# Differential attention of a two-block network: projection groups 1, 6 and 7 run tile by tile beside the sixteen attention units, with the group and output orders changed

## The chip, the cores and the metric

The program runs on one core of one Trainium2 chip. The metric is the device time of one execution in microseconds (us), taken as the median of several executions. The core has TensorE (PE, with its weight loads shown apart as PEld), VectorE (DVE), ScalarE (ACT), GpSimd (POOL) and SyncE (SP, which issues most loads). Each engine works through its own list of instructions in order and waits for the others by semaphores.

## What is computed

The kernel runs two transformer blocks on 256 tokens of width 1024, in float32. The part around the change is the first mixer of the second block. Cut to what matters:

```python
def mixer_ab(hx, hc, w_in, w_out, ...):
    q_x, k_x, v_x, gu_x, gv_x = split(hx @ w_in)      # widths 1024, 1024, 1024, 512, 512
    q_x, k_x = apply_rope(q_x), apply_rope(k_x)       # 8 heads of 2 x 64
    k_c, v_c = split(hc @ w_in[:, 1024:3072])         # 256 context tokens
    k_all, v_all = concat([k_c, k_x]), concat([v_c, v_x])
    s = einsum('bqhmd,bkhmd->bhmqk', q, k) * 64 ** -0.5
    p = softmax(s)
    o_x = (p[:, :, 0] - lam * p[:, :, 1]) @ v         # differential attention, 8 heads
    a_x = head_rms(o_x)                               # width 1024
    u, v = gelu(gu_x), layer_norm(gelu(gv_x))
    g_x = u * (w_s @ v + b_s)                         # the gate, width 512
    return concat([a_x, g_x]) @ w_out                 # 1536 x 1024
```

Ahead of it stands the first block (windowed attention and a gated feed-forward layer); behind it come a layer norm, an expert layer (PEER), a pooling mixer and a second PEER layer. They are the same in both kernels.

## The kernel before

**Products.** A float32 weight tile of 128x1024 is loaded by SP into a `raw` buffer (five of them) and split in two parts: `hilo` (L197 to L200) makes the high part `hi` with an ACT copy (L199) and the rest `lo` with a DVE subtraction (L200; POOL for the few tiles that the plan marks). Each product then takes three matmuls. Weight tiles follow one list, `_plan` (L81). `W.use` (L71) hands out the next tile and, with its default look-ahead of 2, first splits the tiles up to two places further on. So the instructions for splitting a tile are issued when the tile two places before it is used. There are three `hi` and three `lo` buffers.

**The AB projections.** `w_in` is cut into eight groups of 512 columns, four tiles each: 0 and 1 are the queries, 2 and 3 the keys, 4 and 5 the values, 6 and 7 the two halves `gu` and `gv` of the gate. `AB_ORDER` (L117) is their order. `ab_group` (L1044) is a generator that does one tile per step: 24 matmuls of 128x512 for a group with context tokens (2 to 5), 12 for the others. Each step also runs one or two entries of a list `todo` through `do_next` (L1013). `ab_evac` (L1017) puts a finished group's remaining work on that list: the rotary products on DVE and POOL and the transpositions on PE (L988 to L1009) for queries and keys, copies for values, `Gelu` on ACT (L1041) for the gate. `AB_PUMPS` (L114) says in which groups a step also does a piece of `ada`, a modulation product on DVE with a load of its own (L318).

**The gate.** `gate_steps` (L1107) is a generator of seven steps: two loads, a layer norm of `gv` for each half of the tokens on DVE (L508 to L1118), two steps of matmuls and DVE products (L1123, L1125), two of transpositions and splits (L1134).

**The attention.** A loop over `u` from 0 to 21 (L1267) is a software pipeline written out by hand. A unit is one head and one half of the queries. Unit `u` issues, in this order: squares of an earlier head (ACT), `d_scale` of u-1 (reciprocal and product with lambda on DVE L1198, L1199, then a scaled copy on ACT L1200), `d_scores` of u (four passes of matmul into two PSUM banks L1179, two maxima on DVE L1183, L1184), output and norm of earlier heads (`d_out`, `d_on`, L1252 and L1238), `d_mix` of u-1 (DVE L1205), `d_transpose` of u-2 (PE L1212, ACT copy L1214), `d_values` of u-3 (PE L1224), `d_exp` of u (two `Exp` on ACT L1191), and in every other unit `d_flip` (PE L1250). In u from 16 to 21 the attention drains, and eight of the twelve tiles of `w_out` are multiplied there (L240 to L244), in the order of `AB_OUT_ORDER` (L118); the last four follow behind the loop (L267 to L269). All matmul results lie in eight PSUM banks, handed out by the framework as they come free.

Before, seven groups run ahead of the loop, with the gate's steps put on `todo` when group 7 is done, and the last group (1, the queries of heads 4 to 7) runs in units 0 to 3:

```python
for gidx, g in zip(AB_ORDER[:-1], groups):   # L1154
    for _ in g:
        pass
    if gidx == 7:
        gate = gate_steps()
        todo.extend([lambda: next(gate, None)] * 7)
```

Of the kernel before, what the change touches and what calls it, by code (L numbers as in the profile page):

```python
# [2 lines left out]

# [77 lines left out]
def _plan(t):  # L81

    p = [(("q", j), t["att_q"][j], None) for j in range(8)]
    p += [(("o", k), t["att_o"][k], "big" if k >= 8 - O_TAIL else None) for k in range(8)]
    for j in range(FFT):
        p += [(("fi", j, z), t["ffn_in"][z * FFT + j], None) for z in range(2)]
    p += [(("fo", k), t["ffn_out"][k], None) for k in range(FFT)]
    for g in AB_ORDER:
        p += [(("ab", g, k), t["ab_in"][g, k], "pool" if g == AB_ORDER[-1] else None) for k in range(4)]

    p += [(("abo", k), t["ab_out"][k], BIG[AB_OUT_ORDER.index(k) % 2] if k in AB_OUT_ORDER[-TAIL:] else None) for k in AB_OUT_ORDER]
    for li in range(2):
        if li == 1:
            p += [(("pi", k), t["pool_in"][k], "pool" if k == 0 else None) for k in range(8)]
            p += [(("pg", k), t["pool_grp"][k], "big") for k in range(2)]
            p += [(("po", k), t["pool_out"][k], BIG[k % 2] if k >= 8 - TAIL else None) for k in range(8)]
        p += [(("wn", li, k), t["wn"][li, k], "pool" if k == 0 else None) for k in range(8)]
        p += [(("wq", li, g), t["wq"][li, g - 8], "pool" if g in Q_POOL else None) for g in range(8, 16)]

        def u(a, b):  # L100
            return [(("u", li, e), t["u"][li, e], None) for e in range(a, b)]

        def v(a, b):
            return [(("v", li, e), t["v"][li, e], BIG[e % 2] if e >= P - TAIL else None) for e in range(a, b)]

        p += u(0, 112) + v(0, 16) + u(112, 128) + v(16, 128)
    return p


TAIL = 4  # L110
NEXT = 3
O_TAIL = 2
BIG = ("big", "big")
AB_PUMPS = (1,) * 7 + (0,)  # L114
KEEP = 2
ADA_AT = 36
AB_ORDER = (2, 0, 6, 7, 3, 4, 5, 1)  # L117
AB_OUT_ORDER = (8, 9, 10, 11, 0, 1, 2, 3, 4, 5, 6, 7)  # L118
Q_POOL = (9, 12, 15)
Q_ORDER = ((8,), (9, 0), (10, 1), (11, 2), (12, 3), (13, 4), (14, 5), (15, 6, 7), ())  # L120
G_STEP = 1.4
# [3 lines left out]
def tile_two_blocks(ctx: ExitStack, tc: tile.TileContext, t: dict, taps=None):  # L125
# [20 lines left out]
    vec, act, pool, pe, dma = nc.vector, nc.scalar, nc.gpsimd, nc.tensor, nc.sync.dma_start  # L146
# [13 lines left out]
    def mm(shape):  # L160
        n = int(np.prod(shape[1:]))
        v = ps_mm.tile([P, 512], F32, tag="mm", name="mm")[:, 0:n]
        return v.rearrange("p (a b) -> p a b", b=shape[2]) if len(shape) == 3 else v
# [5 lines left out]
    def s1(n=256, dt=F32):  # L169
        return p_s1.tile([P, 512], dt, tag="s1", name="s1")[:, 0:n]  # L170
# [27 lines left out]
    def hilo(src, hi, lo, eng=None):  # L198
        act.activation(out=hi, in_=src, func=AF.Copy)  # L199
        (eng or vec).tensor_tensor(out=lo, in0=src, in1=hi.bitcast(F32), op=OP.subtract)  # L200
# [3 lines left out]
    def split(r, eng):  # L204
# [9 lines left out]
        return hi, lo  # L214

    W = _Weights(_plan(t), load, split)


# [13 lines left out]
    def gemm_n(acc, sT, w, first, last, halves=(0, 1)):  # L232

        (sh, sl), (wh, wl) = sT, w
        cs = [slice(c * 512, c * 512 + 512) for c in range(2)]
        for hf in halves:
            o = acc[hf * 2:hf * 2 + 2]
            tk = slice(hf * P, hf * P + P)
            for c in range(2):
                pe.matmul(o[c], lhsT=sh[:, tk], rhs=wh[:, cs[c]], start=first, stop=False)  # L240
            for c in range(2):
                pe.matmul(o[c], lhsT=sh[:, tk], rhs=wl[:, cs[c]], start=False, stop=False)  # L242
            for c in range(2):
                pe.matmul(o[c], lhsT=sl[:, tk], rhs=wh[:, cs[c]], start=False, stop=last)  # L244

    def ramp(left, tail):

        if tail < TAIL:
            return LOOK if left > tail else left
        return min(left + NEXT - 1, LOOK + max(0, tail + 4 - left))  # L250
# [252 lines left out]
    def ln_stats(src):  # L503
        n = src.shape[-1]
        k = n // 512
        st_ = p_c8.tile([P, 2, 6], F32, tag="st", name="st")
        for i in range(k):
            vec.bn_stats(out=st_[:, i, :], in_=src[:, i * 512:i * 512 + 512])  # L508
        mv = sm(2)
        vec.bn_aggr(out=mv, in_=st_[:, 0:k, :])  # L510
        r = sm(1)
        rsqrt(r, mv[:, 1:2], LN_EPS)
        return mv[:, 0:1], r
# [172 lines left out]
    acc = [mm([P, 512]) for _ in range(2)]  # L686
# [195 lines left out]
    acc = acc_o  # L882
# [75 lines left out]
    acc = [mm([P, 512]) for _ in range(4)]  # L958
# [52 lines left out]
    todo = []  # L1011

    def do_next():  # L1013
        if todo:
            todo.pop(0)()
# [86 lines left out]
    cat = {}  # L1102
# [4 lines left out]
    def gate_steps():  # L1107

        sws = s1(512).rearrange("p (g c) -> p g c", c=P)
        dma(out=sws, in_=t["sgu_w"])  # L1110
        ln = ccrow
        dma(out=ln, in_=t["sgu_ln"].partition_broadcast(P))
        yield
        for hf in range(2):
            mu, rs = ln_stats(gv[:, hf, :])
            vec.tensor_scalar(out=gv[:, hf, :], in0=gv[:, hf, :], scalar1=mu, scalar2=rs, op0=OP.subtract, op1=OP.mult)
            vec.tensor_tensor(out=gv[:, hf, :], in0=gv[:, hf, :], in1=ln[:, 0:512], op=OP.mult)
            vec.tensor_tensor(out=gv[:, hf, :], in0=gv[:, hf, :], in1=ln[:, 512:1024], op=OP.add)  # L1118
            yield
        for hf in range(2):  # L1120
            b = mm([P, 4, P])
            for g in range(4):
                pe.matmul(b[:, g, :], lhsT=sws[:, g, :], rhs=gv[:, hf, g * P:g * P + P], start=True, stop=True)  # L1123
            for g in range(4):
                vec.scalar_tensor_tensor(out=gu[:, hf, g * P:g * P + P], in0=b[:, g, :],  # L1125
                                         scalar=cols[:, C_SGUB + g:C_SGUB + g + 1],
                                         in1=gu[:, hf, g * P:g * P + P], op0=OP.add, op1=OP.mult)
            yield
        for g2 in range(2):
            b = mm([P, 2, NTOK])  # L1130
            for i in range(2):
                g = g2 * 2 + i
                for hf in range(2):
                    pe.transpose(b[:, i, hf * P:hf * P + P], gu[:, hf, g * P:g * P + P], ident)  # L1134
            s = slice(4 + g2 * 2, 6 + g2 * 2)
            hilo(b, c1[:, s, :], c1[:, 8 + s.start:8 + s.stop, :])
            yield

    hT = hT_tiles()
    groups = [ab_group(gidx, pumps, 2 * (gidx == AB_ORDER[0])) for gidx, pumps in zip(AB_ORDER, AB_PUMPS)]  # L1140
    gemm_tail(acc, tail, 0)
# [9 lines left out]
    next(groups[0])  # L1151
    T_out(bs, sc, sh, hT, "ab_hx")

    for gidx, g in zip(AB_ORDER[:-1], groups):  # L1154
        for _ in g:
            pass
        if gidx == 7:
            gate = gate_steps()
            todo.extend([lambda: next(gate, None)] * 7)
        if gidx == 4:  # L1160
            lam_prep()
            iota_f = t4(512)
            dma(out=iota_f, in_=t["iota"])
# [98 lines left out]
    acc = None  # L1262
    c2 = big_T(F32R)[0]
    for i in range(4):
        cat[4 + i] = (c2[:, i, :], c2[:, 4 + i, :])
    ab_out = list(AB_OUT_ORDER)
    for u in range(16 + 6):  # L1267
        if u == 16:
            grow = row_pe(mod2[:, 16:24])
        if u == 7:  # L1270
            while todo:
                do_next()
        if u < 4:
            next(groups[-1])
        elif u < 7:
            do_next()
        if at(u, 5) is not None:
            d_squares(at(u, 5))
        if 0 <= u - 1 < 16:
            d_scale(u - 1)  # L1280
        if u < 16:
            d_scores(u)
        if at(u, 7) is not None:
            d_out(at(u, 7))
        if at(u, 6) is not None:
            d_on(at(u, 6))
        if 0 <= u - 1 < 16:
            d_mix(u - 1)
        if 0 <= u - 2 < 16:
            d_transpose(u - 2)  # L1290
        if 0 <= u - 3 < 16:
            d_values(u - 3)
        if u < 16:
            d_exp(u)
        if at(u, 5) is not None:
            d_rms(at(u, 5))
        for _ in range((2, 2, 1, 1, 1, 1)[u - 16] if u >= 16 else 0):
            if acc is None:
                acc = [mm([P, 512]) for _ in range(4)]
            k = ab_out.pop(0)  # L1300
            gemm_n(acc, cat[k], W.use(("abo", k), ramp(len(ab_out) + 1, TAIL)), k == 8, False)
        if at(u, 6) is not None:
            d_flip(at(u, 6))
    scsh = ln_fold(0, mod2)
# [409 lines left out]
    acc = zacc  # L1714
# [32 lines left out]
    for q in range(2):  # L1747
        wh, wl = [x.rearrange("p (g k e) -> p g k e", k=2, e=NTOK) for x in W.use(("pg", q), 1 - q)]
        for gg in range(2):
            g = q * 2 + gg  # L1750
# [9 lines left out]
    acc = [mm([P, 512]) for _ in range(4)]  # L1760
# [105 lines left out]
```

## Time and profile before

| | us |
|---|---|
| median of 3 executions | 2323.43 |
| lowest, highest | 2318.09, 2325.98 |
| the profiled execution | 2319.79 |
| its span, first to last instruction | 2318.0 |
| last two groups of 12-matmul steps ahead of the keys (6 and 7) | 24.3 |
| from the first scores to the drain (16 units) | 62.6 |
| from the drain to the last four tiles of `w_out` | 27.9 |

A row of the timeline gives start, duration, engine, line, operation and tiles of an instruction; neighbours that are alike are merged (x2 and more). A matmul's duration includes its way through the array, so that matmuls which follow each other overlap, and the distance between two starts is what one costs. On ACT and DVE, too, the next instruction starts a little before the row of the last one ends; the text goes by distances of starts.

### The profile page before, as it was taken

The numbers are of one execution on the slowest core, as the hardware profiler recorded it, in microseconds if no ns is written. First come the engines' busy times: TensorE is split into PE (matmuls) and PEld (weight loads), VectorE is DVE, ScalarE is ACT, GpSimd is POOL, SyncE is SP. The second block draws the span as 40 slices with busy tenths as digits, with TensorE's granted clock in tenths as the row PEclk, the third lists the DMA queues.
The fourth block names the chain that finished last, engine by engine and source line by source line (L and its number), as shares of the span: only waits on it lengthen the run. The fifth ranks groups of instructions, "written<-read, shape, count | busy, mean of one in ns | idle before, by whom it ended". The sixth has DMA issues, their size and how long they took to land. (4 is left out here: it accounts for less than half of the span.)

```text
span 2318.0 us, 37641 instructions
## 1 busy us (share of the span) xinstructions
PE 2235.9 (96%) x14766; PEld 1980.6 (85%) x14766; DVE 1650.6 (71%) x2816; ACT 1161.4 (50%) x1692; POOL 118.8 (5%) x103
## 2 busy tenths in 40 slices
PE   6989999989999999999999999999999999999998
PEld 4669988866799999988888887899999998988886
DVE  3658878646699788776777667779877755566666
ACT  3764444357454555434444445554455544444443
POOL 0000001020400000000000002130000000000001
PEclk8999999999999999999999999999999999999999
DMA  8777786522466687898898766555677777778774
GB/s 329 235 236 254 250 271 225 202 82 59 168 195 188 226 273 256 278 331 266 288 310 287 246 215 226 203 164 187 193 243 241 249 229 220 212 237 249 240 245 154
DMA packets 205057, 531.13 MB, mean 229 GB/s; under 512 B 16496, under 2 KB 84624, under 8 KB 204752
## 3 DMA queue, kind: packets, MB, share of 16 engines
q1 hardware_dynamic: 195632, 495.15, 65.6%
q10 hardware_dynamic: 9248, 33.59, 4.5%
q8 instruction: 115, 1.88, 0.3%
q14 instruction: 62, 0.51, 0.1%
HBM read 491.93 MB, written 36.75 MB: 228 GB/s over the span
## 5 line engine op out<-in xcount | busy, mean ns | idle before, releaser
L200 DVE TENSOR_TENSOR lo<-raw,hi 128x1024 fp32r<-128x1024 f32 x655 | 806.1, 1234 | 469.0 <-ACT hi L199 467.1
L199 ACT ACTIVATE hi<-raw 128x1024 fp32r<-128x1024 f32 x668 | 706.7, 1059 | 791.5 <-PE mm L244 349.0
L225 PE MATMUL mm<-hTh,lo 128*128 128x256 f32 x2592 | 737.2, 284 | 10.8 <-DVE lo L200 8.8
L223 PE MATMUL mm<-hTh,hi 128*128 128x256 f32 x2592 | 746.9, 288 | 0.5 <-ACT hTh L458 0.5
L224 PE MATMUL mm<-hTl,hi 128*128 128x256 f32 x2592 | 735.6, 284 | 0.5 <-DVE hTl L460 0.5
L225 PEld LDWEIGHTS mm<-hTh,lo 128*128 128x128 f32 x2592 | 498.0, 192 | 14.8 <-DVE lo L200 12.3
L223 PEld LDWEIGHTS mm<-hTh,hi 128*128 128x128 f32 x2592 | 498.0, 192 | 2.9 <-issue 2.1
L224 PEld LDWEIGHTS mm<-hTl,hi 128*128 128x128 f32 x2592 | 498.5, 192 | 0.8 <-issue 0.6
L242 PE MATMUL mm<-lo,s 128*128 128x512 f32 x992 | 305.8, 389 | 1.8 <-DVE lo L200 1.7
L240 PE MATMUL mm<-hi,s 128*128 128x512 f32 x992 | 305.6, 389 | 0.0
L244 PE MATMUL mm<-hi,s 128*128 128x512 f32 x992 | 305.5, 389 | 0.0
L242 PEld LDWEIGHTS mm<-lo,s 128*128 128x128 f32 x992 | 186.1, 188 | 41.3 <-DVE lo L200 2.6
L244 PEld LDWEIGHTS mm<-hi,s 128*128 128x128 f32 x992 | 186.1, 188 | 39.0 <-DVE s L200 0.3
L240 PEld LDWEIGHTS mm<-hi,s 128*128 128x128 f32 x992 | 185.8, 188 | 38.4
L1498 ACT ACTIVATE t<-mm 128x512 f32<-128x512 f32 x128 | 75.6, 593 | 90.3 <-DMA gspill<-t 44.5
L1480 DVE TENSOR_TENSOR t<-t,pk 128x1024 f16<-128x1024 f16 x128 | 88.6, 692 | 4.4
L1491 PE MATMUL mm<-t 128*128 128x128 f16 x1024 | 79.6, 220 | 9.7 <-DVE t L1480 9.5
L1477 DVE TENSOR_TENSOR t<-pk,iota 128x1024 f16<-128x1024 f16 x128 | 87.6, 685 | 1.2 <-PE mm L1491 0.7
L200 DVE TENSOR_TENSOR s<-big,s 128x512 fp32r<-128x512 f32 x126 | 86.1, 683 | 0.0
L1523 DVE TENSOR_TENSOR big<-t,big 128x1024 f32<-128x1024 f32 x64 | 77.8, 1218 | 6.0 <-DMA t<-gspill 6.0
L318 DVE SCALAR_TENSOR_TENSOR raw<-raw,t 128x1024 f32<-128x1024 f32 x56 | 68.3, 1220 | 17.0 <-DMA raw<-in_ada_dram 12.6
L200 POOL TENSOR_TENSOR lo<-raw,hi 128x1024 fp32r<-128x1024 f32 x13 | 32.3, 2483 | 900.4 <-ACT hi L199 900.4
(290 smaller groups left out, 2356.9 us busy)
## 6 DMA issues: line engine op xcount, KB each, us to landing
raw<-in_u_dram SPq DMA_DIRECT2D x256, 512.0 KB, 4.3
raw<-in_v_dram SPq DMA_DIRECT2D x256, 512.0 KB, 4.4
raw<-in_ada_dram SPq DMA_DIRECT2D x96, 512.0 KB, 4.6
gspill<-t ACTq DMA_DIRECT2D x64, 512.0 KB, 3.3
t<-gspill SPq DMA_DIRECT2D x64, 512.0 KB, 5.6
raw<-in_ffn_in_dram SPq DMA_DIRECT2D x44, 512.0 KB, 4.4
raw<-in_ada1n_dram SPq DMA_DIRECT2D x32, 512.0 KB, 4.1
raw<-in_ab_in_dram SPq DMA_DIRECT2D x32, 512.0 KB, 4.6
```

The source lines that it names most:

```text
L199: act.activation(out=hi, in_=src, func=AF.Copy)
L200: (eng or vec).tensor_tensor(out=lo, in0=src, in1=hi.bitcast(F32), op=OP.subtract)
L223: pe.matmul(out, lhsT=sh, rhs=mh, start=(i == 0), stop=False)
L224: pe.matmul(out, lhsT=sh, rhs=ml, start=False, stop=False)
L225: pe.matmul(out, lhsT=sl, rhs=mh, start=False, stop=(i == n - 1))
L240: pe.matmul(o[c], lhsT=sh[:, tk], rhs=wh[:, cs[c]], start=first, stop=False)
L242: pe.matmul(o[c], lhsT=sh[:, tk], rhs=wl[:, cs[c]], start=False, stop=False)
L244: pe.matmul(o[c], lhsT=sl[:, tk], rhs=wh[:, cs[c]], start=False, stop=last)
L1477: vec.tensor_tensor(out=o12, in0=pk[:, 0].rearrange("p a q n -> p (a q) n").unsqueeze(2).to_broadcast([P, 4, P, 2]), in1=iota2.unsqueeze(1 ...
L1480: vec.tensor_tensor(out=o[:, 1024:2048].rearrange("p (a q i n) -> p a q i n", q=2, i=P, n=2), in0=o1.to_broadcast([P, 2, 2, P, 2]), in1=pk ...
L1491: pe.matmul(b[:, n, :], lhsT=o[:, 0, a, 1, :, m], rhs=o[:, 1, a, q, :, m], start=q == 0, stop=q == 1)
L1523: vec.tensor_tensor(out=ag, in0=held.pop(("gr", k)), in1=ag, op=OP.mult)
```

## The change

Groups 6 and 7 leave the stage ahead of the loop and run in it, behind group 1: twelve steps, one in each of the units 0, 1, 2, 4, 5, 6, 8, 9, 10, 12, 13 and 14. The gate's steps go to units 15 to 18, two a unit. The tiles of `w_out` for heads 0 to 5 come first, then the four of the gate, then heads 6 and 7. Group 1's `lo` parts go from POOL to DVE, and `ada` is pumped in the first five groups.

```diff
-        p += [(("ab", g, k), t["ab_in"][g, k], "pool" if g == AB_ORDER[-1] else None) for k in range(4)]
+        p += [(("ab", g, k), t["ab_in"][g, k], None) for k in range(4)]
...
-AB_PUMPS = (1,) * 7 + (0,)
+AB_PUMPS = (1,) * 5 + (0,) * 3
...
-AB_ORDER = (2, 0, 6, 7, 3, 4, 5, 1)
-AB_OUT_ORDER = (8, 9, 10, 11, 0, 1, 2, 3, 4, 5, 6, 7)
+AB_ORDER = (2, 0, 3, 4, 5, 1, 6, 7)
+AB_OUT_ORDER = (0, 1, 2, 3, 4, 5, 8, 9, 10, 11, 6, 7)
...
-    for gidx, g in zip(AB_ORDER[:-1], groups):
+    for gidx, g in zip(AB_ORDER[:-3], groups):
         for _ in g:
             pass
-        if gidx == 7:
-            gate = gate_steps()
-            todo.extend([lambda: next(gate, None)] * 7)
...
+    beside = itertools.chain(*groups[-3:])
     for u in range(16 + 6):
...
-        if u < 4:
-            next(groups[-1])
-        elif u < 7:
-            do_next()
+        if u == 15:
+            gate = gate_steps()
+            todo.extend([lambda: next(gate, None)] * 7)
+        if u < 16 and u % 4 < 3:
+            next(beside)
+        else:
+            for _ in range(1 if u < 15 else 2):
+                do_next()
```

What this does to the lists of the engines is shown at three places. Lines of the changed kernel are one higher than before up to the loop, and two lower in it (`Exp` L1191 is L1189, the scaled copy L1200 is L1198, the reciprocal L1198 is L1196).

ACT, around unit 10, from `Exp` of unit 9 on. `t` is a unit's probabilities, `mm` a PSUM bank, `sm` small columns, `big` a long-lived buffer. Before:

```order
L1191 ACTIVATE t_5080,sm<-mm,sm 128x512 x2
L1200 ACTIVATE t_5080<-t_5080,sm 128x512
L1214 ACTIVATE big<-mm 128x512
L1191 ACTIVATE t_5116,sm<-mm,sm 128x512 x2
L1230 ACTIVATE s_5145,sm<-mm 128x128
```

Now:

```order
L1189 ACTIVATE t_4945,sm<-mm,sm 128x512 x2
L1042 ACT_TABLE_LOAD
L1042 ACTIVATE big<-mm 128x512 x2
L200 ACTIVATE hi<-raw 128x1024
L1198 ACTIVATE t_4945<-t_4945,sm 128x512
L1212 ACTIVATE big<-mm 128x512
L1189 ACT_TABLE_LOAD
L1189 ACTIVATE t_5003,sm<-mm,sm 128x512 x2
```

A split's `hi` stands between the `Exp` of one unit and the scaled copy of the same unit (as in each of the units with a step), and in unit 10 the group's `Gelu` as well, with a table load on either side. The same pair of loads stands around the `Gelu` of group 7 in unit 15.

DVE, in units 9 and 10, from the maxima of unit 9 on (`s` holds a head's normed output). Before:

```order
L1183 TENSOR_REDUCE sm<-mm 128x1 x2
L1184 TENSOR_SCALAR sm<-sm 128x2
L200 TENSOR_TENSOR big<-s_5089,big 128x256
L1205 SCALAR_TENSOR_TENSOR t_5043<-t_5043,sm 128x512
L467 TENSOR_SCALAR sm<-sm 128x2
L1198 RECIPROCAL sm<-sm 128x2
L1199 TENSOR_TENSOR sm<-sm,lam 128x1
L1183 TENSOR_REDUCE sm<-mm 128x1 x2
```

Now:

```order
L1181 TENSOR_REDUCE sm<-mm 128x1 x2
L1182 TENSOR_SCALAR sm<-sm 128x2
L201 TENSOR_TENSOR big<-s_4954,big 128x256
L1203 SCALAR_TENSOR_TENSOR t_4890<-t_4890,sm 128x512
L468 TENSOR_SCALAR sm<-sm 128x2
L201 TENSOR_TENSOR lo<-raw,hi 128x1024
L1196 RECIPROCAL sm<-sm 128x2
L1197 TENSOR_TENSOR sm<-sm,lam 128x1
L1181 TENSOR_REDUCE sm<-mm 128x1 x2
```

A split's `lo` now stands ahead of the reciprocal and of the next unit's maxima.

DVE, in unit 16, from the mix of unit 14 on. Before:

```order
L1205 SCALAR_TENSOR_TENSOR t_5262<-t_5262,sm 128x512
L467 TENSOR_SCALAR sm<-sm 128x2
L1198 RECIPROCAL sm<-sm 128x2
L1199 TENSOR_TENSOR sm<-sm,lam 128x1
L1242 TENSOR_SCALAR s_5348<-mm,sm 128x128 x2
L1205 SCALAR_TENSOR_TENSOR t_5299<-t_5299,sm 128x512
L200 TENSOR_TENSOR lo<-raw,hi 128x1024 x2
```

Now:

```order
L1117 TENSOR_SCALAR big<-big,sm 128x512
L1118 TENSOR_TENSOR big<-big 128x512
L1119 TENSOR_TENSOR big<-big 128x512
L1196 RECIPROCAL sm<-sm 128x2
L1197 TENSOR_TENSOR sm<-sm,lam 128x1
L1240 TENSOR_SCALAR s_5316<-mm,sm 128x128 x2
L1203 SCALAR_TENSOR_TENSOR t_5245<-t_5245,sm 128x512
L201 TENSOR_TENSOR lo<-raw,hi 128x1024 x2
L1126 SCALAR_TENSOR_TENSOR big<-mm,cols,big 128x128 x8
```

The whole layer norm of `gv` (its last three rows are shown) now stands between the mix of unit 14 and the reciprocal and mix of unit 15.

## Rows read from the trace of the kernel before

**Rows 1.** The page, part 1: busy us, share of the span, count.

```profile
PE 2235.9 (96%) x14766; PEld 1980.6 (85%) x14766; DVE 1650.6 (71%) x2816; ACT 1161.4 (50%) x1692; POOL 118.8 (5%) x103
```

**Rows 2.** Windows: groups 6 and 7, the sixteen units, the drain.

```profile
core 0: us, PE busy (x) PEld busy (x) DVE busy (x) ACT busy (x) POOL busy (x), PEclk, DMA share, GB/s
393.59:417.88 24.29, 23.66 (x108) 18.73 (x106) 21.12 (x30) 12.55 (x15) 4.84 (x4) 1.00 0.88 307
490.50:553.10 62.60, 50.64 (x280) 32.21 (x280) 47.10 (x120) 48.78 (x127) 11.08 (x11) 0.97 0.12 34
553.10:581.00 27.90, 27.90 (x153) 23.90 (x152) 16.66 (x28) 18.70 (x36) 2.07 (x3) 1.00 0.47 142
```

**Rows 3.** Timeline of PE: start of group 6, a transposition in it, the group after 7.

```profile
393.59 0.47 PE L1059 MATMUL mm<-hi,hTh 128*128 128x512 f32 x1
...
401.88 0.60 PE L1008 MATMUL mm<-kst,t 128*128 128x128 f32 x4
...
417.88 0.39 PE L1059 MATMUL mm<-hi,big 128*128 128x512 f32 x1
```

**Rows 4.** The gate's lines on PE: count, duration in ns, first and last start.

```profile
L1123 PE MATMUL mm<-big,s x16: 270/275/275, 434.3 to 436.0; 128*128 128x128 f32 x16
...
L1134 PE MATMUL mm<-kst,big x8: 271/272/273, 441.5 to 442.3; 128*128 128x128 f32 x8
```

**Rows 5.** Timeline of ACT (units 2 and 3) and of DVE, with a split.

```profile
503.54 0.69 ACT L1191 ACTIVATE t<-mm,sm 128x512 f32<-128x512 f32 x1
...
504.88 1.05 ACT L199 ACTIVATE hi<-raw 128x1024 fp32r<-128x1024 f32 x1
...
508.89 0.69 ACT L1191 ACTIVATE t<-mm,sm 128x512 f32<-128x512 f32 x1
...
505.96 1.23 DVE L200 TENSOR_TENSOR lo<-raw,hi 128x1024 fp32r<-128x1024 f32 x1 [1.81 <-ACT hi L199]
...
507.37 1.28 DVE L1183 TENSOR_REDUCE sm<-mm 128x1 f32<-128x512 f32 x2
```

**Rows 6.** Timeline of ACT, units 12 to 14, without a split.

```profile
542.62 0.69 ACT L1191 ACTIVATE t<-mm,sm 128x512 f32<-128x512 f32 x1
...
544.56 0.72 ACT L1200 ACTIVATE t<-t,sm 128x512 f32<-128x512 f32 x1
545.19 0.46 ACT L1255 ACTIVATE s<-mm,dng 128x256 f32<-128x256 f32 x1
...
546.48 0.68 ACT L1191 ACTIVATE t<-mm,sm 128x512 f32<-128x512 f32 x1
...
549.74 0.69 ACT L1191 ACTIVATE t<-mm,sm 128x512 f32<-128x512 f32 x1
```

**Rows 7.** The line of the units' Exp: first and last start.

```profile
L1191 ACT ACTIVATE t<-mm,sm x32: 677/687/724, 493.3 to 554.3; 128x512 f32<-128x512 f32 x32
```

**Rows 8.** Timeline of PE, unit 3: step, scores, transposition, next scores.

```profile
500.08 0.47 PE L1059 MATMUL mm<-hi,hTh 128*128 128x512 f32 x1
...
503.02 1.13 PE L1179 MATMUL mm<-big 64*128 64x512 f32 x4
504.21 0.66 PE L1212 MATMUL mm<-kst,t 128*128 128x128 f32 x4
...
505.69 1.13 PE L1179 MATMUL mm<-big 64*128 64x512 f32 x4
```

**Rows 9.** Timeline of ACT: the Gelu of group 6 with its table load.

```profile
406.62 1.28 ACT L1041 ACT_TABLE_LOAD   x1
407.91 1.09 ACT L1041 ACTIVATE big<-mm 128x512 f32<-128x512 f32 x2
```

**Rows 10.** DVE: the rotary product's line, the gate's layer norm.

```profile
L997 DVE TENSOR_TENSOR s<-mm,kst x8: 409/416/418, 380.2 to 516.7; 128x256 f32<-128x256 f32 x8
...
L508 DVE BATCH_NORM_STATS2 st<-big x2: 685/686/686, 426.0 to 429.7; 128x6 f32<-128x512 f32 x2
```

**Rows 11.** Timeline of PE: the last values product, behind the fourth output tile.

```profile
568.70 1.05 PE L1224 MATMUL mm<-big 128*128 128x128 f32 x8
```

More of the change, by code (lines that the diff above doesn't have):

```diff
@@ L1 @@
+import itertools
 import math
@@ L1300, in tile_two_blocks @@
             k = ab_out.pop(0)
-            gemm_n(acc, cat[k], W.use(("abo", k), ramp(len(ab_out) + 1, TAIL)), k == 8, False)
+            gemm_n(acc, cat[k], W.use(("abo", k), ramp(len(ab_out) + 1, TAIL)), k == AB_OUT_ORDER[0], False)
         if at(u, 6) is not None:
```

## The prediction

> **What bounds the kernel now.** I read the page first: PE is busy in 96% of the span [rows 1], so a gain has to come from a stretch where it isn't, or where it does avoidable work. The windows by stage show where the change acts [rows 2]. In groups 6 and 7 PE is busy in 23.7 of 24.3 us: that stage is paid by PE, with DVE (21.1) and the loads (88% of the DMA engines) close behind. In the sixteen units PE is at 50.6 of 62.6 us, by rows that overlap, DVE at 47.1 and ACT at 48.8: no engine is full, and the units go at the pace of a chain from engine to engine. In the drain PE is full again. So the idea can only pay if two groups of PE work fit beside the units for less than they cost ahead of them. The timelines of the units show what that takes, below.
>
> **The stage ahead, -26.0.** Group 6 starts at 393.59 and the group behind 7 at 417.88 [rows 3]: 24.3 us. Two transpositions of group 0 lie in it and stay; the row has 0.60 with its way through the array, and I take 0.4 each, so 23.5 go. Ninety-six matmuls at some 0.23 would be 21.8; the rest is waiting, which goes too, since the `ada` products and loads now stand beside steps of 24 matmuls. The gate's PE work also leaves the stage: 16 matmuls from 434.3 to 436.0 and the transpositions from 441.5 to 442.3 [rows 4], 2.5 together. (Eight of sixteen transpositions have rows; the time spans them all.) The scores of unit 0 start 26.0 earlier.
>
> **The units, +20.9.** I measure a unit from `Exp` to `Exp`. Without a split it takes 3.26 (546.48 to 549.74) or, where a head's output is formed as well, 3.86 (542.62 to 546.48) [rows 6]. With a split on DVE it took 5.35 in unit 3 [rows 5], and this is a chain, not a queue on one engine: `Exp` pair 1.34 (503.54 to 504.88), `hi` on ACT 1.08 until `lo` starts (505.96), then 1.41 until the maxima start (507.37; `lo`, reciprocal and product), and 1.52 through the maxima and the negation to the next `Exp` (508.89). The new lists have exactly this order in each of the twelve units with a step. PE is no shorter way: the step's twelve matmuls take 2.94 (500.08 to 503.02), scores, transposition and values 2.67 (503.02 to 505.69) [rows 8], 5.6 together, of which the waits at a unit's end can absorb a little. I take 5.35 and keep 5.6 for the range.
>
> Between `Exp` of unit 0 and of unit 14 lie fourteen periods, eleven with a step:
> - eleven at 5.35: 58.9; units 3, 7 and 11 without a step, 3.26 + 3.86 + 3.86: 11.0;
> - group 1's rotary products, four DVE rows of 0.41 a half [rows 10], overlapping by some 0.07: 1.4. In unit 6 they lie between `lo` and the reciprocal and are paid whole, in unit 5 ahead of `lo`, where 0.3 shows; a copy of a transposed block in unit 7 adds about 0.5: 2.2 in all;
> - units 9 and 13: PE's flip of a head waits for DVE's norm, 0.6 behind the `Exp` of the unit before, takes 0.2, and holds the step (2.94) and the scores behind it; from the scores to the `Exp` are 1.2 (503.02 to 504.21 [rows 8]) and 1.4 of maxima. That is 6.3 against 5.35: 1.8 for both;
> - unit 10: the `Gelu` of group 6. A table load of 1.28, two copies 1.09 with their overlap of 0.1 [rows 9], and a second load ahead of `Exp`, which is longer than DVE's way by 0.9 to 1.3. I take 3.4.
>
> Sum 77.3. Before, `Exp` of unit 0 starts at 493.3 [rows 7] and of unit 14 at 549.74 [rows 6]: 56.4. The units grow by 20.9, against 26.0 saved.
>
> The nearest rows for a table switch are these of the load, 1.28 us, with the next copy 1.29 behind the load's start [rows 9]. The Trainium skill, "ScalarE: Activation LUTs", section "What ACT_TABLE_LOAD costs", gives a drain of about 1.38 us beside the load for every switch of set, and its section on table sets advises against mixing sets as this change does; the rows show no such drain. By the page the four loads would add 4 x 1.38, 5.5 us, to the sum.
>
> **The drain, +8.0.** From `Exp` of unit 14: `Exp` pair 1.34, table load 1.28, `Gelu` of group 7 1.09, squares 0.5, scaled copy 0.63 (544.56 to 545.19), output and its `hi` 0.8 [rows 6, 9]; `lo` of that and the mix of unit 14 on DVE: 6.7. Now DVE does the layer norm of `gv`, which lay beside PE-bound steps before: the second half starts 3.7 behind the first (426.0, 429.7 [rows 10]), 7.4 for both: 14.1. Only then come reciprocal and product (0.3) of unit 15; on ACT its scaled copy (0.63), a copy (0.5), two `hi` (2.1), squares (0.5), output (0.4): 18.5. The transposition of unit 15 needs the PSUM bank that this output empties: 0.5, copy 0.6, values 1.0, two output tiles at 2.8: 26.2. PE has meanwhile had two output tiles and the gate's 1.7 us of matmuls, and stands idle for several us. Before, the fourth tile ended at 568.70 [rows 11], 19.0 behind the `Exp` at 549.74: +7.2. The gate's transpositions add 0.8 in unit 18. From there PE was full [rows 2] and I see no new wait. If DVE's order were harmless here, only the gate's 2.5 of PE would stay; that is the lower end.
>
> **At nothing:** group 1's four `lo` on DVE instead of POOL are in the 5.35. The order of the output tiles puts the gate's behind heads 0 to 5, which are ready by then. The same loads lie in the list; the units had only 12% of the DMA engines busy [rows 2]. Nothing behind the mixer changes its order.
>
> **Sum:** -26.0 + 20.9 + 8.0 = +2.9 on the profiled execution of 2319.8. The median of the runs, 2323.4, is 3.6 above that execution, so I forecast 2326.3, about 2326. No change that is smaller than 0.3% (7.0 us: 2316.4 to 2330.4) could be told from none by a few runs.
>
> **Rivals.**
> 1. *PE fills the units* (faster). If `lo` and the maxima found their place earlier than my chain says, the units would cost what PE needs: 16 x 2.67 + 11 x 2.94 + 1.5 for flips, 76.5, against 62.6, so +13.9; -26.0; and 2.5 of the gate's PE work in the drain: -9.6, 2314. For it: PE is far from full in the units, and its granted clock was 0.97 there [rows 2], below the full 2.4 GHz at times, which denser work may mend. Against: the order is fixed, and unit 3 shows 5.35 with PE ready.
> 2. *The step is paid behind the chain* (slower). A group holds two of eight PSUM banks for five units, two heads' outputs two more, a transposition one. Three are left for scores, which need two a unit, so the scores of a unit wait for the `Exp` of the one before, and on PE the next step stands behind them. Then the other seven steps from unit 4 on take 6.3 as well as units 9 and 13: 7 x 0.95, 6.7 more, 2333. It decides once the mean period of a unit with a step is above some 5.7. Against: the 2.94 of a step fit into the time from scores to `Exp`.
> 3. *Table switches cost double* (slower), as the page has it: 2332. The row ahead of the `Gelu` speaks against it.
> 4. *Forecast*: both halves nearly cancel; its own range is 2320 to 2332.
>
> **How the numbers follow.** Forecast 0.57, rival 1 0.18, rival 2 0.20, rival 3 0.05. Rival 1 is spread over 2310 to 2319 and lies mostly below the bound, with a small end of the forecast: faster 0.17. Slower than 2330.4 are most of rivals 2 and 3 and an end of the forecast: 0.24. The rest, 0.59, is within 0.3%. The range reaches to the middle of rival 1 and past rival 2: 2313 to 2336.
>
> **What would show it.** Right: the first scores near 464.5; `Exp` of unit 14 near 544.6; units with a step at 5.3 to 5.7 with ACT waiting for DVE's L1197 between `hi` and the scaled copy; 8 to 9 us in unit 10; in units 16 and 17 a layer norm on DVE with PE idle before L1248 and before the transposition. Wrong: periods of 4.5, or PE without gaps in units 4 to 14 (rival 1); ACT waiting for the maxima behind late scores in most units (rival 2); a gap at each table load (rival 3); or a first score later than 467, if the stage ahead isn't PE's.

## The result and the profile after

The changed kernel takes 2336.03 us (median of 4 executions, 2327.95 to 2337.84), the kernel before 2323.66 (4 executions). The ratio is 1.0056, with a 95% interval of 1.0037 to 1.0074: slower by about 0.56%. A second series, 12 executions beside 35 of the kernel before, gave 1.0039 (1.0026 to 1.0052). The forecast was 2326, within 0.3%, with 2313 to 2336 as the range. The measured time lies 0.03 us above its upper end: a loss clear of the noise, where the forecast had one too small to tell from none.

The profiled execution of the changed kernel is its fastest, 2327.95 us with a span of 2326.2. Against the profiled one of before (2319.79, span 2318.0) it is 8.2 us longer, and the two traces divide that as follows. The first two rows are the windows of before from the first scores to `Exp` of unit 14 and from there to the first matmul of the tail of `w_out`; the next fence has the same windows of the changed kernel (columns as in [rows 2]).

```profile
490.60:549.74 59.14, 47.71 (x261) 30.27 (x260) 44.35 (x114) 45.45 (x116) 11.03 (x11) 0.97 0.12 36
549.74:580.97 31.23, 30.70 (x168) 25.78 (x169) 19.38 (x35) 22.00 (x46) 2.07 (x3) 1.00 0.42 127
```

```profile
465.40:549.70 84.30, 72.76 (x357) 49.61 (x356) 55.19 (x124) 57.46 (x128) 7.33 (x9) 0.94 0.25 80
549.70:589.54 39.84, 34.39 (x192) 28.48 (x193) 28.10 (x57) 26.68 (x52) 4.03 (x5) 1.00 0.33 108
```

The first scores come 25.2 us earlier (465.4 against 490.6), and `Exp` of unit 14 at the same time as before (549.7). So all that was saved ahead of the units is gone by their end. The drain then adds 8.6 us (39.84 against 31.23), with PE idle for 5.4 of 39.84 where it had idled for 0.5.

| stretch | forecast | measured |
|---|---|---|
| up to the first AB matmul on the block's own tokens (`hTh`) | 0 | +0.8 (364.63, now 365.45) |
| from there to `Exp` of unit 0 | -26.0 | -26.0 |
| `Exp` of unit 0 to `Exp` of unit 14 | +20.9 (77.3 for 56.4) | +25.1 (81.6 for 56.5) |
| from there to the tail | +8.0 | +8.6 |
| the tail to the end | 0 | -0.4 |
| sum | +2.9 | +8.2 |

The units are where the forecast went wrong. The rows of ACT give the start of each `Exp`; here those of units 4 to 6, 9, 10, 14 and 15, with the table loads (start, duration, engine, line, operation, tiles). The time of a unit is that from the `Exp` of the unit before to its own.

```profile
487.99 0.69 ACT L1189 ACTIVATE t<-mm,sm 128x512 f32<-128x512 f32 x1 [0.33 <-DVE sm L1182]
...
495.55 0.69 ACT L1189 ACTIVATE t<-mm,sm 128x512 f32<-128x512 f32 x1 [0.34 <-DVE sm L1182]
...
502.51 0.69 ACT L1189 ACTIVATE t<-mm,sm 128x512 f32<-128x512 f32 x1
...
519.79 0.69 ACT L1189 ACTIVATE t<-mm,sm 128x512 f32<-128x512 f32 x1 [0.24 <-DVE sm L1182]
...
521.25 1.28 ACT L1042 ACT_TABLE_LOAD   x1
...
527.43 1.28 ACT L1189 ACT_TABLE_LOAD   x1
528.72 0.69 ACT L1189 ACTIVATE t<-mm,sm 128x512 f32<-128x512 f32 x1
...
549.71 0.69 ACT L1189 ACTIVATE t<-mm,sm 128x512 f32<-128x512 f32 x1
...
551.18 1.28 ACT L1042 ACT_TABLE_LOAD   x1
...
556.00 1.28 ACT L1189 ACT_TABLE_LOAD   x1
557.30 0.69 ACT L1189 ACTIVATE t<-mm,sm 128x512 f32<-128x512 f32 x1
```

Unit 5 takes 7.56 us (487.99 to 495.55), where the forecast had 5.65. Why is seen on POOL and PE, in the timeline of unit 5 of the same kernel:

```profile
489.78 0.74 POOL L1002 TENSOR_TENSOR t<-t,s 128x256 f32<-128x256 f32 x1 [63.95 <-DVE t L1000]
490.49 1.73 POOL L1003 TENSOR_TENSOR t<-t,s 128x256 f32<-128x256 f32 x1
...
490.29 0.39 PE L1062 MATMUL mm<-hi,hTl 128*128 128x512 f32 x1
492.27 0.66 PE L1009 MATMUL mm<-kst,t 128*128 128x128 f32 x4 [1.60 <-POOL t L1003]
492.86 1.13 PE L1177 MATMUL mm<-big 64*128 64x512 f32 x4
```

The list puts the transposition of group 1's first rotated half (L1009) into the same step as its rotary products, and ahead of the unit's scores (L1177). The rotary product ends with two additions on POOL, the second of which took 1.73 us. PE waited 1.60 us for it, and the scores, the maxima and `Exp` of the unit waited behind.

The second thing on PE is its clock. The windows below lie around two of the places where it fell (an idle stretch, the one behind it, and the next).

```profile
476.50:479.40 2.90, 0.00 (x0) 0.00 (x0) 2.83 (x7) 1.76 (x3) 0.00 (x0) 1.00 0.43 90
481.00:483.50 2.50, 2.50 (x8) 2.02 (x8) 1.72 (x4) 2.31 (x6) 0.00 (x0) 0.50 0.00 0
484.50:487.00 2.50, 2.50 (x14) 1.32 (x13) 2.00 (x4) 0.79 (x2) 0.00 (x0) 1.00 0.10 13
500.80:503.00 2.20, 0.00 (x0) 0.00 (x0) 2.17 (x7) 1.69 (x3) 0.94 (x2) 1.00 0.50 199
504.50:507.00 2.50, 2.50 (x12) 1.74 (x9) 1.61 (x4) 2.47 (x10) 0.00 (x0) 0.50 0.03 7
508.00:510.50 2.50, 2.50 (x13) 1.97 (x11) 1.17 (x2) 1.30 (x3) 0.71 (x1) 1.00 0.00 0
```

Behind an idle stretch PE runs at 0.50, that is 1.2 GHz, for some 3 us, and then at 2.4 GHz again. The mean of the units is 0.94 (0.97 before, where one such stretch lies in them). Unit 4 takes 5.82 and unit 8 6.60 here; in a second trace of the same kernel (e0_after below), where the clock is full in both, 5.35 and 5.41.

In the drain, the rows of DVE and PE show the wait that the forecast described: two layer norms, then the reciprocal of unit 15, and PE idle three times ahead of its flip, the transposition and the values product.

```profile
556.60 0.69 DVE L509 BATCH_NORM_STATS2 st<-big 128x6 f32<-128x512 f32 x1
...
560.37 0.69 DVE L509 BATCH_NORM_STATS2 st<-big 128x6 f32<-128x512 f32 x1
...
564.11 0.16 DVE L1196 RECIPROCAL sm<-sm 128x2 f32<-128x2 f32 x1
...
565.04 0.44 PE L1248 MATMUL mm<-kst,s 128*128 128x128 f32 x2 [1.30 <-DVE s L1240]
...
568.59 0.66 PE L1210 MATMUL mm<-kst,t 128*128 128x128 f32 x4 [1.33 <-ACT s L1253]
...
569.93 1.16 PE L1222 MATMUL mm<-big 128*128 128x128 f32 x8 [0.69 <-ACT big L1212]
```

### The profile page after: what moved, and what is told of

It is laid out like the page before. It is cut to its first block, busy times and chain, and to the rows that moved or that the text cites. A ratio compares the mean times of both kernels' runs of the same rounds, so it can differ in the third digit from the quotient of the medians.

```text
span 2326.2 us, 37652 instructions
## 1 busy us (share of the span) xinstructions
PE 2238.0 (96%) x14766; PEld 1979.6 (85%) x14766; DVE 1653.3 (71%) x2820; ACT 1165.4 (50%) x1695; POOL 113.1 (5%) x99
## 5 line engine op out<-in xcount | busy, mean ns | idle before, releaser
L1494 PE MATMUL mm<-t 128*128 128x128 f16 x1024 | 79.6, 220 | 11.4 <-DVE t L1483 11.4
L319 DVE SCALAR_TENSOR_TENSOR raw<-raw,t 128x1024 f32<-128x1024 f32 x56 | 68.4, 1221 | 16.4 <-DMA raw<-in_ada_dram 12.1
L1555 ACT ACTIVATE big<-mm 128x512 f32<-128x512 f32 x128 | 74.5, 582 | 5.9 <-PE mm L226 5.8
```

The lines of the kernel that those rows point to most:

```text
L1494: pe.matmul(b[:, n, :], lhsT=o[:, 0, a, 1, :, m], rhs=o[:, 1, a, q, :, m], start=q == 0, stop=q == 1)
```

## The experiments

The table has, for one profiled execution of each kernel, the time from `Exp` to `Exp` of the units that matter, from that of unit 0 to that of unit 14, and from there to the tail, all in us as differences of starts. What stands ahead of the AB projections and behind the tail is the same code in all of them, but not the same time: the first AB matmul (on context tokens) starts at 354.2 to 358.4 us in these traces, and from the tail to the end it is 1736.7 to 1743.5. From that matmul to `Exp` of unit 0 the nine traces with the changed order of groups agree within 0.03 us (110.5). So the windows say more of the change than the span of a single execution does.

| kernel | u1 | u4 | u5 | u6 | u8 | u10 | u15 | 0 to 14 | 14 to tail |
|---|---|---|---|---|---|---|---|---|---|
| forecast | 5.35 | 5.35 | 5.65 | 6.75 | 5.35 | 8.75 | | 77.3 | 39.2 |
| changed | 5.36 | 5.82 | 7.56 | 6.96 | 6.60 | 8.93 | 7.59 | 81.6 | 39.8 |
| e0_after | 5.36 | 5.35 | 8.98 | 6.96 | 5.41 | 8.93 | 7.58 | 81.4 | 41.4 |
| e1_gate_behind | 5.35 | 5.35 | 8.99 | 6.95 | 5.41 | 8.93 | 7.59 | 81.4 | 36.6 |
| e2_T_later | 5.35 | 7.05 | 5.69 | 7.11 | 5.41 | 8.93 | 7.58 | 81.0 | 39.8 |
| e3_no_gelu | 5.35 | 5.35 | 8.96 | 6.96 | 6.33 | 6.32 | 4.75 | 81.1 | 38.4 |
| e7_rope_apart | 5.35 | 5.84 | 5.69 | 5.36 | 5.35 | 8.93 | 7.58 | 77.7 | 41.4 |
| e5_one_switch | 5.35 | 5.35 | 5.68 | 5.35 | 5.34 | 6.32 | 3.85 | 74.4 | 36.2 |
| e9_split_alone | 4.02 | 4.09 | 8.09 | 5.41 | 4.61 | 7.19 | 7.58 | 71.2 | 41.4 |
| e6_split_late | 4.02 | 4.09 | 5.82 | 5.24 | 4.45 | 4.41 | 3.84 | 67.3 | 36.2 |

**The changed kernel again.**

> The changed kernel again, for a better interval. In its profiled execution it is 8.2 us longer than the profiled one before (25.2 earlier at the first scores, level at Exp of unit 14, 8.6 later at the first matmul of the tail), while its median so far is 12.4 us above the other's. If the profile holds all of the loss, the ratio lies at 1.003 to 1.004; if executions without that luck lose something more in other stages, at 1.005 or above.

2330.81 us, ratio 1.0039 (1.0026 to 1.0052), profiled span 2329.1. With this series the loss is some 9 us by the ratio and 10.4 by the medians, near the 8.2 of the two traces above. Of the first four executions three (2334.8 to 2337.8) lie near or above the upper end of these twelve (2329.2 to 2335.8), at a mean granted clock of 0.986 to 0.989 where the fourth had 0.991; no trace shows the three, and what made them slower stays open. The trace of e0_after differs from the first in the place of the half clock: unit 5 (8.98) and the drain (41.4) instead of units 4 and 8. Here the idle stretch in unit 5, the stretch behind it, and one in the drain:

```profile
488.80:491.00 2.20, 0.06 (x1) 0.00 (x0) 1.73 (x4) 0.87 (x1) 1.93 (x2) 1.00 0.02 4
491.50:497.50 6.00, 5.94 (x21) 4.11 (x22) 2.21 (x6) 3.46 (x11) 0.49 (x2) 0.50 0.29 87
...
569.50:572.50 3.00, 3.00 (x12) 2.71 (x13) 2.67 (x8) 0.80 (x1) 1.31 (x1) 0.51 0.80 281
```

**The gate behind the output tiles.** The seven steps of the gate stay in units 15 to 18, but from 16 on at the unit's end:

```diff
-        else:
-            for _ in range(1 if u < 15 else 2):
-                do_next()
+        elif u < 16:
+            [do_next() for _ in range(1 if u < 15 else 2)]
...
             gemm_n(acc, cat[k], W.use(("abo", k), ramp(len(ab_out) + 1, TAIL)), k == AB_OUT_ORDER[0], False)
+        [do_next() for _ in range(2 * (u >= 16))]
```

> The gate's steps in units 16 to 18 are issued behind the unit's output tiles instead of ahead of its reciprocal. Theory (the layer norm on DVE holds reciprocal, scaled copy, transposition and PE): T of unit 15 starts some 7 us earlier against Exp of unit 14, the four waits of PE in the drain (1.59, 1.30, 1.33 and 0.69 us, 4.9 together) shrink to under 1.6, and the tail starts 35 to 37 us behind Exp of unit 14 instead of 39.8: 3 to 5 us faster than the changed kernel. Rival (the layer norm only moves: the lo parts of the output tiles now stand behind it on DVE and PE waits for these): under 1 us faster, with waits of the same sum ahead of the output tiles.

2328.24 us, ratio 1.0031 (1.0016 to 1.0046). The intervals of this and of e0_after overlap (2.6 us between the medians), so the total doesn't tell them apart. Nor do the spans, both 2329.1: what lies behind the tail took 5.0 us longer in this execution. The windows do. `Exp` of unit 14 starts at 549.04 in it, and these are its rows of PE in the drain, without a wait ahead of them:

```profile
562.94 0.38 PE L1248 MATMUL mm<-kst,s 128*128 128x128 f32 x2
563.16 0.60 PE L1210 MATMUL mm<-kst,t 128*128 128x128 f32 x4
...
585.65 0.39 PE L268 MATMUL mm<-big 128*128 128x512 f32 x1
```

The transposition of unit 15 stands 14.1 us behind that `Exp` instead of 18.9, and the tail 36.6 instead of 39.8: the 3.2 lie in the expected 3 to 5. The layer norm in front of the reciprocal cost that; the rival, that the wait only moves, is out. The transposition gained 4.8, not 7, since it now waits for `Exp` of unit 15 and its table load.

**The transposition one unit later.**

```diff
-            todo.extend(steps[i] for i in ((0, 2, 1, 3) if gidx == 1 else range(4)))
+            todo.extend([steps[0], lambda: None, lambda: (steps[2](), steps[1]()), steps[3]] if gidx == 1 else steps)
```

> Only the transposition of the first rotated half of group 1 moves, from the step of unit 5 to that of unit 6; DVE and POOL keep their order. Theory (PE waits for POOL's two additions, and the scores of unit 5 and all behind them wait in PE's queue): the period of unit 5 falls from 7.56 to 5.4 to 5.8, unit 6 keeps its 7.0, and Exp of unit 14 comes 1.8 to 2.2 us earlier; with the later flips and steps perhaps 1 more. Rival A (unit 5 is long because of the rotary products on DVE): 7.2 or more stays. Rival B (PSUM banks or PE itself set the pace, and the time comes back later): Exp of unit 14 moves by under 0.7.

Unit 5 falls to 5.69, in the expected 5.4 to 5.8, with POOL's addition as slow as ever (1.74), and unit 6 stays at 7.1: the wait for POOL is the cause of unit 5, and rival A is out. But `Exp` of unit 14 comes hardly earlier against unit 0 (81.0 for 81.4), which is what rival B foresaw, and the time, ratio 1.0059 (1.0040 to 1.0078), is no better. The windows of this kernel show where the time went:

```profile
474.80:477.00 2.20, 0.00 (x0) 0.00 (x0) 2.17 (x5) 1.08 (x2) 0.00 (x0) 1.00 0.33 37
477.50:483.50 6.00, 5.55 (x19) 4.94 (x20) 3.19 (x8) 4.85 (x11) 0.00 (x0) 0.50 0.14 56
484.00:490.00 6.00, 6.00 (x33) 4.30 (x31) 3.96 (x11) 3.64 (x8) 0.53 (x1) 1.00 0.30 90
```

In this execution PE ran at half clock for 6 us in units 3 and 4, and unit 4 took 7.05 instead of 5.35; unit 7, with 3 us at half clock, took 5.58. What the edit gave, the clock took in another place. As a test of the total the run is inconclusive, and alone it does not exclude rival B; e7_rope_apart below, which takes away the same wait and gains 3.7, speaks against it.

**No switch of tables.**

```diff
-                                                func=AF.Gelu_apprx_tanh) for hf in range(2)])
+                                                func=AF.Copy) for hf in range(2)])
```

> The Gelu of groups 6 and 7 is a plain copy here (the gate's activation is left out), so no table is switched among the units. Theory (a load costs its row of 1.28 us and no more): unit 10 falls from 8.93 to some 6.4, unit 15 from 7.59 by 2 to 2.6, 4 to 5 us in all of which the drain may keep 1. Rival, the rule of the Trainium skill, page ScalarE: Activation LUTs, section What ACT_TABLE_LOAD costs (a drain of some 1.38 us beside each load): 2.7 us a load, four loads, 10 us. Second rival (ACT has slack there): under 2 us.

Unit 10 falls from 8.93 to 6.32 and unit 15 from 7.58 to 4.75, by 2.6 and 2.8: two loads of 1.28 each, and hardly more. By the rule of the Trainium skill (ScalarE: Activation LUTs, What ACT_TABLE_LOAD costs) each would have fallen by some 5.3, an estimate from its 2.66 us a switch. The traces show no such drain (`Exp` of unit 10 starts 1.29 behind its load), and the measurement decides. The time is 2326.77, ratio 1.0025 (1.0008 to 1.0043), 4.0 below e0_after by the medians. In the trace `Exp` of unit 14 gains nothing from it (81.1): units 8 and 12 were at half clock in this execution (6.33 and 6.63).

**The rotary halves and their transpositions, one a unit.**

```diff
-            todo.extend(steps[i] for i in ((0, 2, 1, 3) if gidx == 1 else range(4)))
+            todo.extend([steps[0], lambda: None, steps[2], steps[1], steps[3]] if gidx == 1 else steps)
...
-        if u == 7:
-            while todo:
-                do_next()
```

> The changed kernel with only the rotary halves of group 1 and their transpositions in units 5, 6, 7 and 8, one each. Theory (PE's wait for POOL and the rotary rows between lo and reciprocal): unit 5 at 5.4 to 5.7, unit 6 at 5.4, unit 7 up to 5; where PE keeps its full clock, Exp of unit 14 stands 77 to 78.5 us behind that of unit 0. Rival (the time comes back by the clock or the banks): above 80.

Units 5 and 6 take 5.69 and 5.36, and unit 14 stands 77.7 behind unit 0, inside the expected 77 to 78.5. By units, 7.56, 6.96 and 4.40 for units 5 to 7 of the changed kernel become 5.69, 5.36 and 5.05: the order in which it lists the rotary pieces costs 2.8 us. The single time, 2327.38 us, says nothing of the total; as in e0_after the drain took 41.4.

**All three repairs.** The rotary order of e7 and the gate's place of e1, and in unit 10 only a copy:

```diff
-                                                func=AF.Gelu_apprx_tanh) for hf in range(2)])
+                                                func=AF.Copy if gidx == 6 else AF.Gelu_apprx_tanh) for hf in range(2)])
...
-            gate = gate_steps()
-            todo.extend([lambda: next(gate, None)] * 7)
+            gate = gate_steps(); next(gate); todo.append(lambda: act.activation(out=QB[:, 3072:4096], in_=QB[:, 3072:4096], func=AF.Gelu_apprx_tanh))
+            todo.extend([lambda: next(gate, None)] * 6)
```

> Three repairs of the changed kernel together. The rotary halves of group 1 and their transpositions go to units 5, 6, 7 and 8, one each, so that no transposition waits for POOL; group 6 is only copied out of PSUM in unit 10, and the Gelu of both halves of the gate runs in unit 16, behind the last Exp, with one table load in place of four; the gate's other steps stand behind the output tiles. Theory (each loss is a wait in its own place, and they add): unit 5 at 5.4 to 5.7 (7.6 to 9.0 before), unit 6 at 5.4 (7.0), unit 10 at 6.4 (8.9), unit 15 at 4 (7.6), and with 5.4 in the rest Exp of unit 14 stands 75 to 78 us behind that of unit 0 instead of 81.4; the tail 34 to 37 behind Exp of unit 14 plus nothing for the table: 10 to 14 us off the span of the changed kernel, a ratio to the kernel before of 0.997 to 1.000. Rival (PE's drop to half clock after each idle stretch, or PSUM banks, take back what a wait gives): Exp 0 to Exp 14 stays above 79.

2320.24 us, ratio 1.0003 (0.9992 to 1.0015): level with the kernel before, just above the expected 0.997 to 1.000. Against e0_after the median fell by 10.6 and the span by 14.1 (2315.0 for 2329.1), but not all of that is the repairs. Of the 14.1, 6.9 lie in the units and 5.2 in the drain; 3.1 lie ahead of the AB projections, in code that is the same, and 1.1 were lost again behind the tail. Of the 12.1 in the units and the drain some 3 are half clock, which e0_after had in unit 5 and in the drain. So the repairs themselves are worth some 9 us, a little less than the expected 10 to 14; each wait fell in its own place. In these windows (the units, then the drain) the clock is full throughout:

```profile
462.10:539.22 77.12, 68.05 (x357) 46.44 (x356) 54.77 (x124) 54.45 (x127) 7.35 (x9) 1.00 0.28 87
539.22:575.46 36.24, 33.90 (x192) 28.45 (x193) 27.79 (x57) 26.08 (x52) 5.07 (x5) 1.00 0.35 116
```

**The split behind the mix, alone.** The parts of the next tile are made later in the unit, so that on DVE `lo` stands behind the maxima instead of ahead of the reciprocal, and on ACT `hi` ahead of `Exp`:

```diff
             d_mix(u - 1)
+        if u < 14 and u % 4 < 3: W.ahead(3)
```

> The changed kernel with the split behind the mix as its only edit. Theory (hi, lo, reciprocal and maxima in one chain make a unit with a step 5.35 long): units 1, 2, 12 and 14 fall to between 4 and 5, units 5 and 6 keep a wait for POOL or the rotary rows, unit 10 keeps most of its 8.9 by the two table loads; Exp of unit 14 stands 74 to 78 us behind that of unit 0 instead of 81.4. Rival (PE or the scores' PSUM banks set the 5.35): 80 or more.

2322.65 us, ratio 1.0003 (0.9988 to 1.0017). With this one line `Exp` of unit 14 comes 10.2 us earlier against unit 0 (71.2 for 81.4), more than expected; 1.4 of it is the half clock that e0_after had in unit 5 (8.98 against 7.56). The rows of ACT from `Exp` of unit 0 to that of unit 1:

```profile
468.16 0.69 ACT L1189 ACTIVATE t<-mm,sm 128x512 f32<-128x512 f32 x1 [1.52 <-DVE sm L1182]
...
470.09 0.72 ACT L1198 ACTIVATE t<-t,sm 128x512 f32<-128x512 f32 x1 [0.48 <-DVE sm L1197]
470.72 1.04 ACT L200 ACTIVATE hi<-raw 128x1024 fp32r<-128x1024 f32 x1
472.18 0.69 ACT L1189 ACTIVATE t<-mm,sm 128x512 f32<-128x512 f32 x1 [0.41 <-DVE sm L1182]
```

The scaled copy now waits 0.5 us for DVE and not for `lo`, where it had waited 1.6 in the changed kernel, and units 1, 2, 4 and 12 fall to between 4.0 and 4.2. So there 5.35 was the chain's length and not PE's; unit 14 falls only to 5.24, where 4 to 5 was expected. Unit 10, at 7.19, keeps the loads, and unit 5, at 8.09, the wait for POOL:

```profile
486.74 0.72 POOL L1002 TENSOR_TENSOR t<-t,s 128x256 f32<-128x256 f32 x1 [60.84 <-DVE t L1000]
487.42 0.72 POOL L1003 TENSOR_TENSOR t<-t,s 128x256 f32<-128x256 f32 x1
...
488.19 0.66 PE L1009 MATMUL mm<-kst,t 128*128 128x128 f32 x4 [1.69 <-POOL t L1003]
```

Here DVE's `lo` stands ahead of the rotary rows, both additions are quick, and PE waits 1.69 us all the same. So it is the order (rotary rows, additions and transposition ahead of the scores) that holds unit 5, and not the slow addition.

**Everything, and the kernel before with what fits it.** e6_split_late adds to e5_one_switch the line above, and moves a head's flip behind the next unit's scores:

```diff
         if at(u, 7) is not None:
+            if u < 17: d_flip(at(u, 7))
             d_out(at(u, 7))
...
-        if at(u, 6) is not None:
+        if at(u, 6) is not None and u >= 16:
             d_flip(at(u, 6))
```

> As the kernel with one switch, and in the units the split of a weight tile stands behind the mix (hi ahead of Exp on ACT, lo behind the maxima on DVE), and a head is flipped behind the next unit's scores. Theory (a unit with a step is as long as its chain through hi, lo, reciprocal and maxima, 5.35, while PE needs 5.3 by its rows: 2.94 for the step, 1.06 scores, 0.49 transposition, 0.81 values): the chain falls to about 4 and PE becomes the bound, so units with a step stay at 5.3, but units 9 and 13 fall from 6.3 to 5.5 and unit 10 to 5.3: 2 to 4 us less than with one switch alone. Rival (the scores wait for the Exp of the unit before for want of PSUM banks): units of 5.5 to 6 and no gain.

2312.01 us, ratio 0.9959 (0.9946 to 0.9972): faster than both kernels, by 0.4% than the one before. `Exp` 0 to 14 is 67.3, 7.1 less than in e5_one_switch, where 2 to 4 were expected. Units 1 and 2 account for 2.6 of it: PE has no transposition or values product ahead of their scores, so it needs 4.0 for each and not the 5.3 that was counted. Units 9 and 13 were expected at 5.5 and stay long (6.46 and 6.15), and the units behind them are shorter than the expected 5.3 instead (4.41 and 4.42). The windows show what bounds the whole:

```profile
464.90:534.91 70.01, 68.33 (x359) 47.00 (x360) 54.99 (x124) 54.12 (x127) 6.29 (x9) 1.00 0.33 102
534.91:571.11 36.20, 33.98 (x192) 28.40 (x193) 27.75 (x57) 26.08 (x52) 5.07 (x5) 1.00 0.33 103
```

PE is busy in 68.3 of 70.0 us: this is rival 1 of the prediction, reached by another order.

> The kernel before with the two edits of e6_split_late that fit it: in units 0 to 2 the split stands behind the mix, and a head is flipped behind the next unit's scores. It tells whether the gain of that kernel needs the groups beside the units. Theory (the groups beside are worth it once the waits are gone): this one gains 1 to 4 us in the units (periods of 5.35 fall to 4.0 to 5.3 in units 1 to 3, the flips take 0.6 from a few units), ratio 0.998 to 1.000, and e6_split_late stays 5 us or more faster. Rival (the edits alone make the gain): 0.996 or below.

In the kernel before, the same two edits (the split in units 0 to 2) give 2316.59 us, ratio 0.9985 (0.9971 to 0.9999): 3.5 us by the ratio and 4.9 by the medians, where 1 to 4 were expected. `Exp` 0 to 14 is 50.9 for 56.5, with no stretch at half clock in it, but `Exp` of unit 0 comes 2.1 later behind the first scores (4.8 for 2.7), since POOL's `lo` parts now hold up DVE ahead of it (last section). From the first AB matmul on `hTh` to the tail the gain is 3.8 (212.5 for 216.3), within the expected. The groups beside the units are worth the rest of what e6_split_late gains: 4.6 us between the two medians, which are of two series, 6.0 by the two ratios, and 6.4 between the traces (206.1 for 212.5).

## Why the prediction missed

**The stage ahead, -26.0: right**, to 0.1 us. PE paid for groups 6 and 7 there, and the nine traces agree on this stage.

**A unit with a step, 5.35: right**, for the reason given. Units 1, 2 and 14 take 5.35 to 5.41, and e9_split_alone shows for 1 and 2 that the chain makes them so. Also right are units 9 and 13 (6.28 and 6.34 for 6.3, the flip) and unit 10 (8.93 for 8.75, the loads).

**The drain, +8.0: right** (+8.6), with the steps of its path: the reciprocal of unit 15 was put 14.1 behind `Exp` of unit 14 and stands at 14.4, the transposition at 18.5 and stands at 18.9. e1_gate_behind shows that the layer norm's place costs 3.2 of it. The lower end, that only the gate's 2.5 us of PE work would stay with DVE's order harmless, was too low: in e1_gate_behind 5.4 stay (36.6 against 31.2), 3.5 of them busy time of PE and 1.9 idle.

**The step that failed** is the second term of the units, "group 1's rotary products ... 2.2 in all". It counted four DVE rows a half and the copy on ACT. It left out POOL's two additions, and that in PE's list the transposition that waits for them stands ahead of the scores of unit 5. That is 1.9 us (7.56 for 5.65), shown by the row of PE's wait and by e2_T_later and e7_rope_apart, where unit 5 takes 5.69.

**The clock was left out of the sum.** Rival 1 even hoped that denser work would mend it. The work is denser, but PE's waits are fewer and longer: six from the first scores to `Exp` of unit 14, 11.4 us in all, three of them of 2.3 to 3.3 us, where the kernel before has ten, 10.5 in all, two of them of 2.3 and 2.8. The clock fell behind all three, and the units lost 1.7 us to it (0.47 in unit 4, 1.2 in unit 8), by comparison with the same units of e0_after. The two make 3.6 of the 4.2 by which the units missed; the rest is small (0.2 each in units 6 and 10).

**Rival 2** (PSUM banks, periods of 6.3 in all later units) did not happen, though its time was near: units 12 and 14 take 5.45 and 5.35. Its time came from other places.

**The bound.** With +8.2 in place of +2.9 the sum lies at 2331.6, just past the 0.3%; of these 5.3 us the units are 4.2 and the drain 0.6. The other 4.4 of the 9.7 us missed are in the step from the profiled execution to the median: the forecast took it at 3.6 as before, and it was 8.1 in the first series. In the second the profiled execution lies on the median (2330.91 and 2330.81), so these 4.4 are a spread of executions whose cause is not shown, and that the time left the range by 0.03 us is due to them.

## What to carry to other kernels

When work is put beside a chain that alternates between engines, ask of each moved instruction which link of the chain it now stands in front of: the two instructions of a split, 1.0 us on ACT and 1.2 on DVE, placed behind the maxima and the mix instead of ahead of the reciprocal, were worth 8 to 10 us over eleven units here. Follow a moved item through every engine to its last consumer: a transposition that waits for an addition on POOL holds all that stands behind it in PE's list. Where a gain of one place does not appear in the total, look at the clock of the stretches beside it, and at the time of the parts that did not change, before giving up the cause.

## What was not expected of the hardware

PE's granted clock falls to 1.2 GHz for 3 to 6.5 us behind some of its idle stretches of 2 to 3.3 us, and not always the same ones. The idle time ahead of the transposition in unit 3 was 3.28 us in the first execution of the changed kernel, and the clock fell behind it; in the second (e0_after) it was 3.27 and did not, but fell behind the wait in unit 5. Such a stretch cost between nothing (the third, in units 10 and 11) and 1.7 us (unit 4 of e2_T_later, 7.05 for 5.35). No run here settles what decides. In e5_one_switch and e6_split_late none lies between the first scores and the tail, although PE idled 3.27 us in unit 3 of the former too.

POOL's addition L1003 took 1.73 us in unit 5 and 0.72 in unit 6, with the same shapes. In unit 5 it started at 490.49, just behind DVE's `lo` (490.42, 1.22 us long), and ended 0.6 behind it. The Trainium skill (SBUF — State Buffer, section "SBUF: two separate sides") has a port pair that VectorE and GpSimd hold in turn, each for a whole instruction. Of VectorE's instructions it names those with two inputs in SBUF, as `lo` has, among others. The rows agree with it. In e9_split_alone, where `lo` runs before the additions, L1003 takes 0.72 us in unit 5 as well. The traces show the same the other way round: DVE's negation ahead of `Exp` (L1184, 0.17 us in most units) took 1.08 us in unit 1 of the kernel before, and in unit 0 of e8_before_late 2.25 us, to the end of POOL's `lo` parts (489.17 and 4.73 us):

```profile
489.17 4.73 POOL L200 TENSOR_TENSOR lo<-raw,hi 128x1024 fp32r<-128x1024 f32 x2 [4.50 <-ACT hi L199]
...
491.67 2.25 DVE L1184 TENSOR_SCALAR sm<-sm 128x2 f32<-128x2 f32 x1
```
